# Rotary embedding, 16 x 512 x 1024: loading x ahead of the tables, and the last tile computed and stored in four pieces

## Chip, cores, metric

The kernel runs on one core of a Trainium2 chip. The metric is device time in microseconds (us); the other cores are idle. The profile's span (the length of the profiled execution) is some 2 us shorter than the time.

## The reference

```python
x = x.reshape(batch, seq, num_heads, head_dim)        # 16, 512, 16, 64, float32
x1, x2 = x[..., :half_dim], x[..., half_dim:]         # half_dim = 32
cos = cos[None, :, None, :]; sin = sin[None, :, None, :]   # 512 x 32 each
return np.concatenate([x1 * cos - x2 * sin, x1 * sin + x2 * cos], axis=-1)
```

It reads 33.6 MB of x, writes as much, and does little arithmetic on each element.

## The kernel before

Each of the 16 batches is one tile: 128 partitions x 4096 elements, four rows of x to a partition (J = 4). SyncE (SP) issues the loads, ScalarE (ACT) casts x to bf16 and issues the stores, VectorE (DVE) does two bf16 multiplies (by cos, by sin), a subtract and an add that write fp32.

```python
xpool: bufs=3   xbpool: bufs=2   mpool: bufs=2   opool: bufs=3      # abridged
nc.sync.dma_start(out=cos_f, in_=cos_v)
nc.scalar.dma_start(out=sin_f, in_=sin_v)
nc.vector.tensor_copy(out=cos_b, in_=cos_f)      # to bf16
nc.vector.tensor_copy(out=sin_b, in_=sin_f)
# ... cut: views ...
for b in range(batch):
    xt = xpool.tile([P, F], fp32, name="xt")
    nc.sync.dma_start(out=xt, in_=x_v[b])
    xb = xbpool.tile([P, F], bf16, name="xb")
    nc.scalar.copy(out=xb, in_=xt)
    # m1, m2 (bf16) and ot (fp32) are allocated
    nc.vector.tensor_tensor(out=full_view(m1), in0=full_view(xb), in1=bcast(cos_b), op=MULT)
    nc.vector.tensor_tensor(out=full_view(m2), in0=full_view(xb), in1=bcast(sin_b), op=MULT)
    nc.vector.tensor_tensor(out=half_view(ot, 0), in0=half_view(m1, 0), in1=half_view(m2, 1), op=SUB)
    nc.vector.tensor_tensor(out=half_view(ot, 1), in0=half_view(m1, 1), in1=half_view(m2, 0), op=ADD)
    nc.scalar.dma_start(out=out_v[b], in_=ot)
```

The program text does not fix the order in which ACT gets its casts and stores. The framework that builds the program arranges them (called the built order below).

## Time and profile before

| | before |
|---|---|
| time, median of 5 runs | 168.29 us (168.24 to 168.73) |
| span of the profiled run | 166.5 us |
| DVE / ACT busy | 142.4 / 58.9 us |
| moved by DMA | 67.25 MB, 404 GB/s over the span |

DVE is busy for 86% of the span, and the DMA engines are full from about 2 to 148 us, at 429 GB/s from 4 us on. The lines are in the prediction.

### The profile page before, as it was taken

The page shows a single profiled execution, that of the slowest core. Times are in us where ns is not written, and L with a number is a line of the kernel's source. Part 1 is how long each engine was busy: PE and PEld are TensorE (multiplying, and loading weights), DVE is VectorE, ACT ScalarE, POOL GpSimd, SP SyncE. Part 2 cuts the span into 40 slices and gives each one's busy share as a digit, 9 for nine tenths or more (in the row PEclk, how much of TensorE's full clock was granted, in tenths as well). Part 3 has the DMA queues.
Part 4 walks back from the last instruction along what each step waited for, and adds up shares of the span by engine and source line. Part 5 has one row for each costly group of instructions (what it writes and reads, how often), then busy time and mean ns, then how long its engine had stood idle before and what let it go on. Part 6 is the DMA issues. An engine that isn't in the chain of part 4 may idle for free.

```text
span 166.5 us, 216 instructions
## 1 busy us (share of the span) xinstructions
DVE 142.4 (86%) x66; ACT 58.9 (35%) x17; POOL 0.2 (0%) x4
## 2 busy tenths in 40 slices
DVE  0009999999999998199999999999999999999920
ACT  3076646153440000978080700533526080800000
POOL 0000000000000000000000000000000000000000
DMA  5999999999999999999999999999999999997455
GB/s 157 429 433 429 429 425 370 433 441 429 421 417 441 441 433 441 429 409 429 441 441 433 429 441 401 437 439 433 437 429 417 425 441 441 433 386 323 189 252 252
DMA packets 4897, 67.25 MB, mean 404 GB/s; under 512 B 544, under 2 KB 800, under 8 KB 800
## 3 DMA queue, kind: packets, MB, share of 16 engines
q1 hardware_dynamic: 2448, 33.62, 48.0%
q10 hardware_dynamic: 2448, 33.62, 47.3%
q14 instruction: 1, 0.01, 0.0%
HBM read 33.69 MB, written 33.55 MB: 404 GB/s over the span
## 4 chain that ended last, share of the span: by engine, by line
DVE 71%; issue 13%; DMA 5%; ACT 4%; DVEq 1%; SPq 0%; ACTq 0%
DVE ot L92 19%; DVE ot L86 19%; DVE m L80 17%; DVE m L83 16%; DMA xt<-in_x_dram 5%; ACT xb L74 4%; DVEq L129 1%; SPq L49 0%; ACTq L98 0%; DVEq L86 0%; ACTq L74 0%
## 5 line engine op out<-in xcount | busy, mean ns | idle before, releaser
L74 ACT CAST xb<-xt 128x4096 bf16<-128x4096 f32 x16 | 57.6, 3605 | 85.5 <-DVE ot L92 50.5
L80 DVE TENSOR_TENSOR m<-xb,cos_b 128x4096 bf16<-128x4096 bf16 x16 | 36.6, 2285 | 13.6 <-ACT xb L74 13.6
L86 DVE TENSOR_TENSOR ot<-m,m 128x2048 f32<-128x2048 bf16 x16 | 36.6, 2289 | 0.3
L92 DVE TENSOR_TENSOR ot<-m,m 128x2048 f32<-128x2048 bf16 x16 | 36.6, 2285 | 0.0
L83 DVE TENSOR_TENSOR m<-xb,sin_b 128x4096 bf16<-128x4096 bf16 x16 | 36.6, 2284 | 0.0
L53 DVE CAST cos_b<-cos_f 128x128 bf16<-128x128 f32 x1 | 0.2, 227 | 2.9 <-DMA cos_f<-in_cos_dram 2.9
L74 ACT ACT_TABLE_LOAD x1 | 1.3, 1283 | 1.1 <-PEq L115 1.1
L54 DVE CAST sin_b<-sin_f 128x128 bf16<-128x128 f32 x1 | 0.2, 228 | 0.0
L115 POOL MEMSET const-bfloat16-1.0<- 128x1 bf16 x1 | 0.1, 101 | 0.0
L115 POOL MEMSET const-uint8-127<- 128x1 uint8 x1 | 0.1, 101 | 0.0
L115 POOL MEMSET const-float32-0.0<- 128x1 f32 x1 | 0.1, 98 | 0.2 <-issue 0.2
L115 POOL MEMSET const-float32-1.0<- 128x1 f32 x1 | 0.1, 98 | 0.0
## 6 DMA issues: line engine op xcount, KB each, us to landing
xt<-in_x_dram SPq DMA_DIRECT2D x16, 2048.0 KB, 18.9
out_dram<-ot ACTq DMA_DIRECT2D x16, 2048.0 KB, 14.8
sin_f<-in_sin_dram ACTq DMA_DIRECT2D x1, 64.0 KB, 2.3
cos_f<-in_cos_dram SPq DMA_DIRECT2D x1, 64.0 KB, 2.1
```

The source lines that it names most:

```text
L53: nc.vector.tensor_copy(out=cos_b, in_=cos_f)
L54: nc.vector.tensor_copy(out=sin_b, in_=sin_f)
L74: nc.scalar.copy(out=xb, in_=xt)
L80: nc.vector.tensor_tensor(out=full_view(m1), in0=full_view(xb), in1=bcast(cos_b), op=MULT)
L83: nc.vector.tensor_tensor(out=full_view(m2), in0=full_view(xb), in1=bcast(sin_b), op=MULT)
L86: nc.vector.tensor_tensor(out=half_view(ot, 0), in0=half_view(m1, 0), in1=half_view(m2, 1), op=SUB,)
L92: nc.vector.tensor_tensor(out=half_view(ot, 1), in0=half_view(m1, 1), in1=half_view(m2, 0), op=ADD,)
L115: nc = _bacc.Bacc("TRN2", target_bir_lowering=False, num_devices=1)
L129: with _tile.TileContext(nc) as tc:
```

## The change

It parametrizes the kernel (J and the buffer counts are unchanged: 4; 3, 2, 2, 3) and is meant to have two effects: the first x load is issued ahead of the cos load, so that the first cast may start sooner, and the last tile is computed and stored in four pieces, so that most of its store lies beside its arithmetic. The diff, cut to these (the comments are added here):

```diff
-    nc.sync.dma_start(out=cos_f, in_=cos_v)
-    nc.scalar.dma_start(out=sin_f, in_=sin_v)
+    pending = load_x(*plan[0])          # the first x load
+    build_tables(Jt_first)              # cos on SP, sin on ACT, and their casts
+    build_tables(J)                     # J = Jt_first = 4: returns at once
...
+        if i == len(plan) - 1:
+            for j in range(J):
+                def piece(v, j=j):
+                    return v[:, j:j + 1]
+                TT = nc.vector.tensor_tensor
+                TT(out=piece(full_view(m1, Jt)), in0=piece(full_view(xb, Jt)), in1=bcast(cb[Jt][t][:, j * half:(j + 1) * half], 1), op=MULT)
+                TT(out=piece(full_view(m2, Jt)), in0=piece(full_view(xb, Jt)), in1=bcast(sb[Jt][t][:, j * half:(j + 1) * half], 1), op=MULT)
+                TT(out=piece(half_view(ot, 0, Jt)), in0=piece(half_view(m1, 0, Jt)), in1=piece(half_view(m2, 1, Jt)), op=SUB)
+                TT(out=piece(half_view(ot, 1, Jt)), in0=piece(half_view(m1, 1, Jt)), in1=piece(half_view(m2, 0, Jt)), op=ADD)
+                nc.scalar.dma_start(out=out_v[b, t][:, j * dim:(j + 1) * dim], in_=ot[:, j * dim:(j + 1) * dim])
+            continue
```

More of the change, by code (lines that the diff above doesn't have):

```diff
@@ L7 @@
 from concourse._compat import with_exitstack
+J = 4
+X_BUFS = 3
+XB_BUFS = 2
+M_BUFS = 2
+O_BUFS = 3
 @with_exitstack
@@ L31 @@
     P = nc.NUM_PARTITIONS
-    assert seq % P == 0
-    J = seq // P
-    F = J * dim
-    x_v = x.rearrange("b (p j) k -> b p (j k)", j=J)
-    out_v = out.rearrange("b (p j) h d -> b p (j h d)", j=J)
-    cos_v = cos.rearrange("(p j) d -> p (j d)", j=J)
-    sin_v = sin.rearrange("(p j) d -> p (j d)", j=J)
-    consts = ctx.enter_context(tc.tile_pool(name="consts", bufs=1))
-    xpool = ctx.enter_context(tc.tile_pool(name="xpool", bufs=3))
-    xbpool = ctx.enter_context(tc.tile_pool(name="xbpool", bufs=2))
@@ L44 @@
-    mpool = ctx.enter_context(tc.tile_pool(name="mpool", bufs=2))
-    opool = ctx.enter_context(tc.tile_pool(name="opool", bufs=3))
-    cos_f = consts.tile([P, J * half], fp32, name="cos_f")
-    sin_f = consts.tile([P, J * half], fp32, name="sin_f")
-    nc.sync.dma_start(out=cos_f, in_=cos_v)
-    nc.scalar.dma_start(out=sin_f, in_=sin_v)
-    cos_b = consts.tile([P, J * half], bf16, name="cos_b")
-    sin_b = consts.tile([P, J * half], bf16, name="sin_b")
-    nc.vector.tensor_copy(out=cos_b, in_=cos_f)
@@ L54, with make_views @@
-    nc.vector.tensor_copy(out=sin_b, in_=sin_f)
-    def bcast(t):
+    assert seq % (P * J) == 0
+    nst = seq // (P * J)
+    def make_views(Jt):
+        x_v = x.rearrange("b (t p j) k -> b t p (j k)", p=P, j=Jt)
+        out_v = out.rearrange("b (t p j) h d -> b t p (j h d)", p=P, j=Jt)
+        cos_v = cos.rearrange("(t p j) d -> t p (j d)", p=P, j=Jt)
+        sin_v = sin.rearrange("(t p j) d -> t p (j d)", p=P, j=Jt)
+        return x_v, out_v, cos_v, sin_v
+    consts = ctx.enter_context(tc.tile_pool(name="consts", bufs=1))
@@ new lines, with build_tables @@
+    xpool = ctx.enter_context(tc.tile_pool(name="xpool", bufs=X_BUFS))
+    xbpool = ctx.enter_context(tc.tile_pool(name="xbpool", bufs=XB_BUFS))
+    mpool = ctx.enter_context(tc.tile_pool(name="mpool", bufs=M_BUFS))
+    opool = ctx.enter_context(tc.tile_pool(name="opool", bufs=O_BUFS))
+    xv = {}
+    cb = {}
+    sb = {}
+    def build_tables(Jt):
+        if Jt in cb:
+            return
+        x_v, out_v, cos_v, sin_v = make_views(Jt)
+        xv[Jt] = (x_v, out_v)
+        n_t = seq // (P * Jt)
+        cb[Jt] = []
+        sb[Jt] = []
+        for t in range(n_t):
+            cf = consts.tile([P, Jt * half], fp32, name=f"cos_f{Jt}_{t}")
+            sf = consts.tile([P, Jt * half], fp32, name=f"sin_f{Jt}_{t}")
+            nc.sync.dma_start(out=cf, in_=cos_v[t])
+            nc.scalar.dma_start(out=sf, in_=sin_v[t])
+            cbt = consts.tile([P, Jt * half], bf16, name=f"cos_b{Jt}_{t}")
+            sbt = consts.tile([P, Jt * half], bf16, name=f"sin_b{Jt}_{t}")
+            nc.vector.tensor_copy(out=cbt, in_=cf)
+            nc.vector.tensor_copy(out=sbt, in_=sf)
+            cb[Jt].append(cbt)
+            sb[Jt].append(sbt)
@@ L57, in bcast @@
+    def bcast(t, Jt):
         return bass.AP(
@@ L59, in bcast, with full_view, half_view @@
             offset=t.offset,
-            ap=[list(t.ap[0]), [half, J], [0, nh * 2], [1, half]],
+            ap=[list(t.ap[0]), [half, Jt], [0, nh * 2], [1, half]],
         )
-    def full_view(t):
-        return t.rearrange("p (j e d) -> p j e d", j=J, e=2 * nh, d=half)
-    def half_view(t, which):
-        v = t.rearrange("p (j h two d) -> p j h two d", j=J, h=nh, two=2)
+    def full_view(t, Jt):
+        return t.rearrange("p (j e d) -> p j e d", j=Jt, e=2 * nh, d=half)
+    def half_view(t, which, Jt):
+        v = t.rearrange("p (j h two d) -> p j h two d", j=Jt, h=nh, two=2)
@@ L68, in half_view, with schedule @@
         return v[:, :, :, which, :]
-    for b in range(batch):
-        xt = xpool.tile([P, F], fp32, name="xt")
-        nc.sync.dma_start(out=xt, in_=x_v[b])
-        xb = xbpool.tile([P, F], bf16, name="xb")
-        nc.scalar.copy(out=xb, in_=xt)
-        m1 = mpool.tile([P, F], bf16, name="m1")
-        m2 = mpool.tile([P, F], bf16, name="m2")
-        ot = opool.tile([P, F], fp32, name="ot")
+    def schedule(Jt_first):
+        seq_tiles = []
+        for b in range(batch):
+            Jt = Jt_first if b == 0 else J
+            n_t = seq // (P * Jt)
+            for t in range(n_t):
+                seq_tiles.append((b, Jt, t))
+        return seq_tiles
@@ new lines, with load_x @@
+    Jt_first = 4
+    plan = schedule(Jt_first)
+    def load_x(b, Jt, t):
+        x_v = make_views(Jt)[0]
+        xt = xpool.tile([P, Jt * dim], fp32, name="xt")
+        nc.sync.dma_start(out=xt, in_=x_v[b, t])
+        return xt
+    pending = load_x(*plan[0])
+    build_tables(Jt_first)
+    build_tables(J)
+    for i, (b, Jt, t) in enumerate(plan):
+        Ft = Jt * dim
+        out_v = xv[Jt][1]
+        xt = pending if i == 0 else load_x(b, Jt, t)
+        xb = xbpool.tile([P, Ft], bf16, name="xb")
+        nc.scalar.copy(out=xb, in_=xt)
+        m1 = mpool.tile([P, Ft], bf16, name="m1")
+        m2 = mpool.tile([P, Ft], bf16, name="m2")
+        ot = opool.tile([P, Ft], fp32, name="ot")
+        if i == len(plan) - 1:
[9 more added lines that the diff above has]
+            continue
@@ L80 @@
         nc.vector.tensor_tensor(
-            out=full_view(m1), in0=full_view(xb), in1=bcast(cos_b), op=MULT
+            out=full_view(m1, Jt), in0=full_view(xb, Jt), in1=bcast(cb[Jt][t], Jt), op=MULT
         )
         nc.vector.tensor_tensor(
-            out=full_view(m2), in0=full_view(xb), in1=bcast(sin_b), op=MULT
+            out=full_view(m2, Jt), in0=full_view(xb, Jt), in1=bcast(sb[Jt][t], Jt), op=MULT
         )
         nc.vector.tensor_tensor(
-            out=half_view(ot, 0),
-            in0=half_view(m1, 0),
@@ L89 @@
-            in1=half_view(m2, 1),
+            out=half_view(ot, 0, Jt),
+            in0=half_view(m1, 0, Jt),
+            in1=half_view(m2, 1, Jt),
             op=SUB,
@@ L92 @@
         nc.vector.tensor_tensor(
-            out=half_view(ot, 1),
-            in0=half_view(m1, 1),
-            in1=half_view(m2, 0),
+            out=half_view(ot, 1, Jt),
+            in0=half_view(m1, 1, Jt),
+            in1=half_view(m2, 0, Jt),
             op=ADD,
         )
-        nc.scalar.dma_start(out=out_v[b], in_=ot)
+        nc.scalar.dma_start(out=out_v[b, t], in_=ot)
 _INS = ['x', 'cos', 'sin', 'num_heads']
```

## The prediction

> **What bounds the kernel now.** I read the page first, for shares of the span, then the chain of waits and the instruction timeline, because shares of a whole run hide stages. The diff keeps the tile (J is 4 before and after, so each of the 16 batches is still one 128x4096 tile) and all buffer counts. So only three places can change: the start, the order in which the engines get their instructions, and the last tile.
>
> ```profile
> DVE 142.4 (86%) x66; ACT 58.9 (35%) x17; POOL 0.2 (0%) x4
> DVE  0009999999999998199999999999999999999920
> DMA  5999999999999999999999999999999999997455
> ```
> These are lines of the page. VectorE (DVE) has work from slice 3 (12.8 us) on with one hole at slice 16, and the DMA engines are full from the second slice to about 150 us. Both are near their limit. The last slices differ: DVE has stopped and DMA is at about half. That is one transfer with nothing beside it.
>
> ```profile
> L74 ACT CAST xb<-xt 128x4096 bf16<-128x4096 f32 x16 | 57.6, 3605 | 85.5 <-DVE ot L92 50.5
> L80 DVE TENSOR_TENSOR m<-xb,cos_b 128x4096 bf16<-128x4096 bf16 x16 | 36.6, 2285 | 13.6 <-ACT xb L74 13.6
> L86 DVE TENSOR_TENSOR ot<-m,m 128x2048 f32<-128x2048 bf16 x16 | 36.6, 2289 | 0.3
> ```
> These groups give a tile's cost: four DVE operations of about 2.29 us each. DVE idles 13.6 us before L80: 9.5 at the start (the first cast) and 4.1 in the middle.
>
> ```profile
> 1.15 8.01 DMA xt<-in_x_dram
> 9.18 3.61 ACT xb L74
> 12.82 2.29 DVE m L80
> ```
> These, from the chain that ended last, are the start: the first x load, the first cast, the first multiply. The load is issued at 1.15, after the cos load's issue (0.73 to 1.10 on the same queue), and lands 8.0 us later. Cos and sin landed by 3.05 us and were not waited for by the multiply.
>
> ```profile
> 63.85 2.28 DVE L92 TENSOR_TENSOR ot<-m,m 128x2048 f32<-128x2048 bf16 x1
> 66.60 7.11 ACT L74 CAST xb<-xt 128x4096 bf16<-128x4096 f32 x2 [19.06 <-DVE ot L92]
> 70.24 2.29 DVE L80 TENSOR_TENSOR m<-xb,cos_b 128x4096 bf16<-128x4096 bf16 x1 [4.11 <-ACT xb L74]
> ```
> This is the hole, from the timeline. The x load of that tile was issued at 29.95 us, and no load took over 23.2 us, so its data had long landed; its buffer was free at about 52.7. The cast stands behind two stores in ACT's queue, and the second waits for the last DVE operation of the tile before. So it is the order of ACT's instructions, fixed when the kernel is built, that costs 4.1 us. From 70.24 on DVE never waits again.
>
> ```profile
> 148.06 2.29 DVE L92 TENSOR_TENSOR ot<-m,m 128x2048 f32<-128x2048 bf16 x1
> 150.27 2.28 DVE L80 TENSOR_TENSOR m<-xb,cos_b 128x4096 bf16<-128x4096 bf16 x1
> 150.38 9.27 ACTq L98 DMA_DIRECT2D out_dram<-ot  x2
> 152.47 2.28 DVE L83 TENSOR_TENSOR m<-xb,sin_b 128x4096 bf16<-128x4096 bf16 x1
> 154.79 2.29 DVE L86 TENSOR_TENSOR ot<-m,m 128x2048 f32<-128x2048 bf16 x1
> 157.00 2.29 DVE L92 TENSOR_TENSOR ot<-m,m 128x2048 f32<-128x2048 bf16 x1
> ```
> This is the end: the last tile's four operations run to 159.28 and only then is its whole 2 MB store issued. Its landing time is the shortest of all stores, 6.3 us, so it lands at 165.6, and the span ends 0.9 us later. Windows of the trace say that DMA moved nothing from 156 to 160 us and then 2.1 MB. So the end is bound by DVE and then by an exposed store.
>
> **What the Trainium skill says.** First, VectorE: DVE Perf Modes, section "The TRN2 errata", says that an operation on SBUF data pays a fixed cost per instruction, and gives (N+151)/0.96 ns for an fp32 tensor_tensor. For N = 2048 that is 2291 ns; the page here has 2289, so it agrees. The timeline adds that an independent next operation starts about 0.08 us before the end of the one ahead (148.06 + 2.29 = 150.35 against 150.27), and one that needs the result just made starts about 0.03 us after (152.47 + 2.28 = 154.75 against 154.79). Second, DMA: Bandwidth & Descriptors, section "Anatomy of one DMA", fits about 2.0 us plus bytes at 436 GB/s, for the GpSimd path. For 2.1 MB that is 6.8 us; the lone last store took 6.3, so the fixed part here looks nearer 1.4. Third, the same page, "Queues, rings and completion order": each engine takes a queue's descriptors in ring order. So a cos load issued behind x would arrive at about the time of x; the trace of before has it the other way round and cannot show this. Fourth, Perfetto Trace Analysis, "DMA Optimizations": splitting a DMA may let some of it start sooner if the DMA engines are idle. They are, from 156 to 160 us.
>
> **The change part by part.** (a) The start: x is issued first and cos behind it. The x load moves from 1.15 to 0.73 us, 0.42 earlier. The cos load should land about when x does, near 9 us, and its two casts of 0.23 us each then lie beside ACT's 3.6 us cast of x, so nothing new is waited for. The whole DVE chain follows by 0.42, since later loads have slack: only the first three casts ever waited for a load. Worth -0.4.
>
> (b) The middle: the same instructions, shapes and buffers. Worth 0 if ACT's order stays.
>
> (c) The last tile on DVE: 16 operations of a quarter size instead of 4. By the skill's formula with N = 512 (bf16 multiplies count two per cycle: 1024/2 = 512) each lasts (512+151)/0.96 = 691 ns, and the next starts after 0.61 if independent and after 0.72 if it needs the one just before. Tile 15 starts at 150.27 - 0.42 = 149.85. If another piece's multiply is put between the sin multiply and the subtract (the order before does this between tiles, at 23.96 to 28.36 us), only the last subtract waits: 14 x 0.61 + 0.72 + 0.69 = 9.95 us. If not, 11 x 0.61 + 4 x 0.72 + 0.69 = 10.28 us. DVE ends at 159.8 to 160.1, say 159.95: 0.7 us later than before, in spite of the earlier start.
>
> (d) The last store: four of 0.52 MB. The store of tile 14 is issued at about 150 and empties by about 156. Pieces 0 to 2 come ready about every 2.5 us (153, 155, 158) and need some 1.2 us each at 430 GB/s, so they are out before piece 3. Piece 3 is alone. Its landing, an estimate: 6.3 us less 1.57 MB at 430 GB/s (3.66) = 2.64; with the skill's fixed part of 2.0 it is 3.2. I take 2.75, as the 64 KB cos load took 2.1 and so the fixed part is no larger than that. End: 159.95 + 0.03 + 2.75 + 0.9 = 163.6, against 166.5: -2.9. In time: 168.29 - 2.9 = 165.4 us, which is 1.7% faster.
>
> **The rivals.** First, the built order changes. Moving the cos load and adding 12 operations may lead the scheduler to another order of casts and stores on ACT. The profile can't say which. If the 4.1 us hole disappears, DVE ends that much earlier; the DMA engines have then to move 67.25 MB at some 430 GB/s, 156 us from 2 us on, so a little of it is lost to DMA: 161 to 162 us. If a second such hole opens, 169. For a steady order speaks that tiles 1 to 14 are written as before; against it, that a hole like this one depends on which of two instructions was ready first in the plan. I give 15% to a better and 7% to a worse order.
>
> Second, the split stores may be held up: if the store of a piece were taken to read the whole output tile, the next piece's subtract would wait for it, and compute and transfer would run in turn, 4 x (2.5 + 2.7) = 21 us after 149.85: 172 us in the trace and 173.5 in time. Against it: L86 and L92 write interleaved halves of one tile, and L92 starts 0.08 us before L86 ends, so disjoint parts are not held apart. 3%.
>
> Third, the quarter-size operations may cost more than thought, or 4 KB rows of a store move more slowly than the 16 KB rows of before. Each 0.1 us per operation is 1.6 us. That would leave 166 to 167 us.
>
> Fourth, the cos load may land after the first cast ends (12.4 us). It would have to take over 11 us for its 64 KB; x's 2 MB take 8. Unlikely, and worth at most 1 us.
>
> **Range and chances.** With the order unchanged (78%) I expect 164.8 to 166.2, centre 165.4; the 2% line is at 164.9, so some 15% of that case is beyond it. Adding nearly all of the better order's 15% gives 0.27 for faster by over 2%, 0.05 for slower and 0.68 between. The 80% range, stretched to the fast side for the first rival, is 162.8 to 166.7.
>
> **What would show it right or wrong.** Right: the first x load issued near 0.73 and the first multiply at about 12.4; the hole of some 4 us before a cast still there at about 66 us; 16 operations of about 690 ns at the end and DVE finishing near 160; four stores of 512 KB with the last landing in 2.6 to 3.2 us. Wrong: a missing or second hole (first rival), subtracts that wait for DMA in the last tile (second), pieces well over 0.7 us (third), or a wait for cos before the first multiply (fourth).

## The result, and the profile after

The changed kernel takes 163.25 us (median of 8 runs, 163.16 to 163.31) against 168.73 (15 runs, 168.24 to 169.37; the five of the table above are among them). The ratio is 0.9678, 95% interval 0.9662 to 0.9694: faster by 3.2%. Ratios in this document are the mean time of one kernel's fast runs over that of the other's in the same rounds, so they are not quite the ratio of the medians quoted.

First the page of the changed kernel: the same three rows as shown of before.

```profile
DVE 143.5 (89%) x78; ACT 59.0 (37%) x17; POOL 0.2 (0%) x4
DVE  0019999999999999999999999999998997999990
DMA  5999999999999999999999999999999999999994
```

The hole of DVE at slice 16 is gone, and the DMA row is full to its last slice but one. There are new small dips of DVE late, at slices 30 and 33 (counted from 0). The view of waits names them (who waited for whom: us in total, times, longest):

```profile
DVE m L137 <- ACT xb L119: 3.0, 1, 3.0
DVE ot L143 <- DMA out_dram<-ot: 1.6, 2, 0.8
```

DVE's only wait for a cast is now the first; in its place come two waits for a store to free an output buffer. Before had no such wait.

The start, from the chain that ended last (start, us, what):

```profile
0.73 8.02 DMA xt<-in_x_dram
8.75 0.02 issue
8.78 3.61 ACT xb L119
12.39 0.02 issue
12.41 2.29 DVE m L137
```

The load takes 8.02 us, as before, from an issue 0.42 us earlier, and the first multiply moves from 12.82 to 12.41.

Where the hole was, from the timeline (start, us, engine, line, operation):

```profile
57.38 3.61 ACT L119 CAST xb<-xt 128x4096 bf16<-128x4096 f32 x1 [5.33 <-DVE ot L149]
...
63.56 2.29 DVE L149 TENSOR_TENSOR ot<-m,m 128x2048 f32<-128x2048 bf16 x1
65.77 2.28 DVE L137 TENSOR_TENSOR m<-xb,cos_b 128x4096 bf16<-128x4096 bf16 x1
```

The cast that this multiply needs was done at 61.0, long before the tile ahead of it was finished. In the built program ACT's queue has another order (c5 is the cast of tile 5, s5 its store; tiles are numbered from 0):

```
before:  c0 c1 c2 s0 c3 s1 c4 s2 c5 s3 s4 s5 c6 c7 c8 s6 c9 s7 c10 s8 s9 c11 s10 c12 ...
after:   c0 c1 c2 s0 c3 s1 c4 s2 s3 c5 s4 c6 s5 c7 s6 c8 s7 c9 s8 c10 s9 c11 s10 c12 ...
```

Before, c6 stood behind s5, which waits for all of tile 5 on DVE; so DVE had nothing of tile 6 when it finished tile 5. After, c6 stands behind s4. The starts of casts and stores in ACT's timelines of both traces follow these two orders.

The end, from the timeline:

```profile
147.71 0.68 DVE L130 TENSOR_TENSOR m<-xb,cos_b 128x1024 bf16<-128x1024 bf16 x1
147.82 0.34 ACTq L155 DMA_DIRECT2D out_dram<-ot  x1
...
150.83 7.09 ACTq L134 DMA_DIRECT2D out_dram<-ot  x4
...
155.53 0.69 DVE L131 TENSOR_TENSOR m<-xb,sin_b 128x1024 bf16<-128x1024 bf16 x1
156.25 0.69 DVE L132 TENSOR_TENSOR ot<-m,m 128x512 f32<-128x512 bf16 x1
156.86 0.68 DVE L133 TENSOR_TENSOR ot<-m,m 128x512 f32<-128x512 bf16 x1
```

The last tile takes 147.71 to 157.54, 9.83 us. Independent operations start 0.60 us apart (147.71 to 148.31); only the last subtract, which nothing could be put in front of, starts 0.72 after the one ahead. The four issues stretch from 150.83 to 157.92. Two windows of the changed trace (the columns are window, its length, busy us and instructions of DVE, ACT and POOL, clock, DMA share, GB/s):

```profile
148.00:156.00 8.00, 8.00 (x14) 0.00 (x0) 0.00 (x0) 1.00 0.99 419
156.00:158.00 2.00, 1.51 (x3) 0.00 (x0) 0.00 (x0) 1.00 1.00 408
```

The 4 us without a transfer, 156 to 160 us in the trace of before, are filled.

So three things moved together: the start, the order on ACT, and the last tile.

### The profile page after: what moved, and what is told of

Read it like the earlier page. It is cut to its first block, busy times and chain, and to the rows that moved or that the text cites. A ratio compares the mean times of both kernels' runs of the same rounds, so it can differ in the third digit from the quotient of the medians.

```text
span 161.5 us, 230 instructions
## 1 busy us (share of the span) xinstructions
DVE 143.5 (89%) x78; ACT 59.0 (37%) x17; POOL 0.2 (0%) x4
## 3 DMA queue, kind: packets, MB, share of 16 engines
q1 hardware_dynamic: 2448, 33.62, 49.4%
## 4 chain that ended last, share of the span: by engine, by line
DVE 67%; DMA 20%; issue 8%; ACT 2%; DVEq 0%
DVE ot L143 18%; DVE m L140 15%; DVE ot L149 15%; DMA out_dram<-ot 15%; DVE m L137 12%; DMA xt<-in_x_dram 5%; ACT xb L119 2%; DVE ot L132 2%; DVE m L130 2%; DVE m L131 2%; DVE ot L133 1%; DVEq L186 0%; DVEq L143 0%
## 5 line engine op out<-in xcount | busy, mean ns | idle before, releaser
L137 DVE TENSOR_TENSOR m<-xb,cos_b 128x4096 bf16<-128x4096 bf16 x15 | 34.3, 2285 | 3.0 <-ACT xb L119 3.0
L143 DVE TENSOR_TENSOR ot<-m,m 128x2048 f32<-128x2048 bf16 x15 | 34.4, 2291 | 2.0 <-DMA out_dram<-ot 1.6
L149 DVE TENSOR_TENSOR ot<-m,m 128x2048 f32<-128x2048 bf16 x15 | 34.3, 2285 | 0.0
L140 DVE TENSOR_TENSOR m<-xb,sin_b 128x4096 bf16<-128x4096 bf16 x15 | 34.3, 2285 | 0.0
L132 DVE TENSOR_TENSOR ot<-m,m 128x512 f32<-128x512 bf16 x4 | 2.7, 686 | 0.0
L131 DVE TENSOR_TENSOR m<-xb,sin_b 128x1024 bf16<-128x1024 bf16 x4 | 2.7, 685 | 0.0
L133 DVE TENSOR_TENSOR ot<-m,m 128x512 f32<-128x512 bf16 x4 | 2.7, 684 | 0.0
L130 DVE TENSOR_TENSOR m<-xb,cos_b 128x1024 bf16<-128x1024 bf16 x4 | 2.7, 684 | 0.0
```

The source lines that it names most:

```text
L130: TT(out=piece(full_view(m1, Jt)), in0=piece(full_view(xb, Jt)), in1=bcast(cb[Jt][t][:, j * half:(j + 1) * half], 1), op=MULT)
L131: TT(out=piece(full_view(m2, Jt)), in0=piece(full_view(xb, Jt)), in1=bcast(sb[Jt][t][:, j * half:(j + 1) * half], 1), op=MULT)
L132: TT(out=piece(half_view(ot, 0, Jt)), in0=piece(half_view(m1, 0, Jt)), in1=piece(half_view(m2, 1, Jt)), op=SUB)
L133: TT(out=piece(half_view(ot, 1, Jt)), in0=piece(half_view(m1, 1, Jt)), in1=piece(half_view(m2, 0, Jt)), op=ADD)
L137: nc.vector.tensor_tensor(out=full_view(m1, Jt), in0=full_view(xb, Jt), in1=bcast(cb[Jt][t], Jt), op=MULT)
L140: nc.vector.tensor_tensor(out=full_view(m2, Jt), in0=full_view(xb, Jt), in1=bcast(sb[Jt][t], Jt), op=MULT)
```

## The experiments

**Theory.** The gain is the sum of an earlier start (0.4 us), another order on ACT that closes the hole (and is a side effect of moving the load), and a last store that is hidden. The closed hole, 4.1 us of DVE, is not worth 4.1 us, because DVE then meets the limit of the DMA engines. **Rivals.** The split changed the order; or the earlier load itself closes the hole; or DVE still bounds the changed kernel. The first four runs were taken together, against 168.27 us of before (11 runs).

### Split alone

The kernel of before with the last tile in pieces (the diff's loop), cos still first. In the built program ACT's order up to the pieces is that of before.

> Only the last tile is split; cos is still loaded first, and the built order of casts and stores on ACT is that of before. Theory (the gain is a sum of two parts: the exposed last store, and the hole that the moved load closes): the hole of about 4.1 us near 66 us stays; the last tile starts at 150.3, takes 9.8 us as in the changed kernel, its last store lands in about 2.7 us, span 163.7, 2.8 us less than before (ratio about 0.983). Rival (the order of ACT was changed by the split): the hole is gone and most of the 5 us gain is here (ratio about 0.968).

165.72 us, ratio 0.9851 (0.9829 to 0.9873); span 163.7. From its timeline and from the view of its output's stores:

```profile
66.29 7.11 ACT L82 CAST xb<-xt 128x4096 bf16<-128x4096 f32 x2 [19.05 <-DVE ot L112]
69.92 2.29 DVE L100 TENSOR_TENSOR m<-xb,cos_b 128x4096 bf16<-128x4096 bf16 x1 [4.11 <-ACT xb L82]
```
```profile
DMA to landing us min/median/max: 2.6/14.7/19.5
```

The hole of 4.11 us is there and the last piece lands in 2.6 us. The split is worth 1.5% by itself and did not change the order.

### x first alone

```diff
+    xt0 = xpool.tile([P, F], fp32, name="xt")
+    nc.sync.dma_start(out=xt0, in_=x_v[0])
     nc.sync.dma_start(out=cos_f, in_=cos_v)
...
+        if b == 0:
+            xt = xt0
+        else:
```

> Only x is loaded ahead of cos; the last tile is whole. In the built program ACT's casts and stores stand in the order of the changed kernel. Theory: no hole at 66 us; DVE ends near 156.6 with some 1.6 us of waits for output buffers, the last 2 MB store is exposed for 6.3 us, span about 163.8, 2.7 us less than before (ratio about 0.984). Rival (moving the load is worth only its 0.4 us of issue): ratio 0.997.

165.76 us, ratio 0.9836 (0.9812 to 0.9860); span 164.0. No hole; DVE's waits for an output buffer are 1.7 us, and the whole last store is exposed again (6.3 us to landing). A move of one issue by 0.4 us gives 1.6%.

### The new order alone

The kernel of before, cos first and the last tile whole, with edges between instructions (order only, no wait) that hold ACT's queue in the order of the changed kernel.

```diff
+    order = "c0 c1 c2 s0 c3 s1 c4 s2 s3 c5 s4 c6 s5 c7 ...".split()
+    for one, two in zip(order, order[1:]):
+        one, two = act[one[0], int(one[1:])], act[two[0], int(two[1:])]
+        tc.add_manual_dep(two.ins, one.ins.name, mybir.DependencyInfo(
+            mybir.DependencyClass.NoSync, mybir.DependencyReason.DATA), reason="act order")
```

> The kernel of before with cos first and the last tile whole, but ACT's casts and stores forced into the order of the changed kernel. Theory (the order is what closes the hole, not the earlier issue): nearly all of the gain of the run with x first, about 0.4 us less of it: span about 164.2, ratio about 0.986. Rival (the earlier start shifts the loads so that the hole closes by itself): ratio 1.00.

166.16 us, ratio 0.9872 (0.9850 to 0.9894). Its profiled execution has a span of 164.8, of which some 0.7 us is a first x load that landed later than in the profile of before (first cast at 9.90 against 9.18). No hole; two waits for output buffers, 1.5 us. The order by itself, with no load moved, is worth 1.3%.

### x first with the old order

The kernel with x first alone, with ACT's queue held in the order of before.

> x is loaded ahead of cos, the last tile is whole, and ACT's casts and stores are forced into the order of before. Theory: the hole of 4.1 us stays, everything starts 0.4 us earlier: 0.4 us less than before, ratio 0.9975. Rival (the earlier load is what counts): ratio about 0.984, as with x first alone.

168.03 us, ratio 0.9980 (0.9963 to 0.9996). The hole is back:

```profile
69.83 2.29 DVE L86 TENSOR_TENSOR m<-xb,cos_b 128x4096 bf16<-128x4096 bf16 x1 [4.10 <-ACT xb L80]
```

So the earlier issue is worth about 0.2 to 0.4 us, and the rest of what x first brought is the order. By the ratios: 1.5% (split) + 1.3% (order) + 0.2% (earlier issue) = 3.0%, against the measured 3.2%; each of the three has an uncertainty of about 0.2%.

### Less DVE work in the changed kernel

The next three runs shared the runs of before (168.38 us). Here ACT's order is held, and in tiles 4 to 11 a copy stands in place of the sin multiply; the result is wrong.

```diff
-        nc.vector.tensor_tensor(out=full_view(m2, Jt), in0=full_view(xb, Jt), in1=bcast(sb[Jt][t], Jt), op=MULT)
+        if 4 <= i < 12:
+            nc.vector.tensor_copy(out=m2, in_=xb)
+        else:
+            ...  # as before
```

> The changed kernel with its ACT order held, and in tiles 4 to 11 a plain bf16 copy in place of the sin multiply (wrong result on purpose), which should take about 1.2 us in place of 2.3 and so about 9 us of DVE work away. Theory (the changed kernel is at the limit of the DMA engines, 67.26 MB at about 430 GB/s from 2 us on, which is 156 us): DVE waits for buffers or data instead, and the span falls by at most 1.5 us. Rival (DVE is still the bound): the span falls by about 8 us, to 153 to 154.

163.33 us, against 163.25 of the changed kernel (of other rounds; the ratios to before are 0.9703 here and 0.9678 there, whose intervals overlap; the next run, of the same rounds as this one and with all of its DVE work, took 163.31). The copy took 1.22 us, so 8.5 us of DVE work are gone (135.0 busy in place of 143.5), and the time did not move. Its waits:

```profile
DVE ot L148 <- DMA out_dram<-ot: 10.3, 7, 1.9
```

1.6 us of waiting for output buffers have become 10.3: 8.7 us more, all that was saved. DVE does not bound the changed kernel.

### Four output buffers

`O_BUFS = 4` in the changed kernel; nothing else.

> The changed kernel with four output buffers in place of three. Theory (DMA is the limit): DVE's two waits for an output buffer (1.6 us) go and DVE ends near 156, but the stores left over queue and the end moves by 0.5 us or less. Rival (DVE and its waits set the end): 1.6 us less, span 159.9.

163.31 us, ratio 0.9706 (0.9691 to 0.9720). The two waits are gone and DVE finishes at about 156, but the pieces of the last store now take 5.8 us to land (median) where they took 4.1. What waits is only moved from DVE to the queue of stores.

### First tile in pieces

A try for a faster version: cos and sin first again, the first tile loaded, cast and computed in four pieces, four output buffers, and a regular order on ACT (c0 c1 s0 c2 s1 c3 s2 ...).

```diff
+        if b == 0:
+            for j in range(J):
+                jj = slice(j * dim, (j + 1) * dim)
+                nc.sync.dma_start(out=xt[:, jj], in_=x_v[b, t][:, jj])
...
+                if i == 0:
+                    nc.scalar.copy(out=xb[:, jj], in_=xt[:, jj])
```

> The changed kernel with cos and sin ahead again, the first tile loaded, cast and computed in four pieces, four output buffers and a regular order on ACT; a try for a faster version. DVE can start near 5 us in place of 12.4. Theory (DMA is the limit): the 7 us are lost to waits for loads and buffers, and the span falls by 0.5 to 1.5 us to about 160 to 161. Rival (DVE is the limit): the span falls by over 5 us.

164.27 us, ratio 0.9766 (0.9744 to 0.9788): 1.0 us slower than the changed kernel, where the theory expected a small gain. DVE starts at 7.2 (not near 5, as expected) and ends at 155.1 us, earlier than in any other kernel with the right result, and it doesn't help, which speaks for the DMA limit. The direction of the small difference was a miss. Two windows of its trace:

```profile
2.00:4.00 2.00, 0.41 (x2) 0.45 (x1) 0.00 (x0) 1.00 0.95 199
4.00:6.00 2.00, 0.00 (x0) 0.00 (x0) 0.00 (x0) 1.00 0.93 338
```

From 2 to 6 us the DMA engines are marked as busy but move 199 and 338 GB/s, against 281 and 442 in the same windows of before (0.37 MB less); these are the tables and the first 512 KB pieces. The kernel to compare with is the changed one: its windows from 0 to 6 us add up to 1.48 MB and those of this run to 1.11, again 0.37 MB less. At 430 GB/s that is an estimated 0.9 us of a DMA-bound kernel, about what was lost. Whether the small rows or the order of the loads is to blame was not taken apart.

### Fewer bytes, then both cuts

The last two runs shared runs of before at 168.32 us. Both hold ACT's order and store only half of each of tiles 4 to 11, so 8.4 MB less; the second also has the copy in place of the sin multiply. Their outputs are wrong, which doesn't matter for the times.

```diff
-        nc.scalar.dma_start(out=out_v[b, t], in_=ot)
+        kk = slice(0, (Ft // 2 if 4 <= i < 12 else Ft))
+        nc.scalar.dma_start(out=out_v[b, t][:, kk], in_=ot[:, kk])
```

> The changed kernel with its ACT order held, and only half of each of tiles 4 to 11 stored (wrong result on purpose): 8.4 MB less, which is 19.5 us of DMA at 430 GB/s. Theory (DMA and DVE are within about 2 us of each other in the changed kernel): DVE's two waits for output buffers (1.6 us) go, DVE ends near 155.9 and bounds at once, the last store lands 2.6 us after: span about 159.5, 2 us less. Rival (DMA alone bounds, DVE has much room): far more than 2 us less.

161.71 us, ratio 0.9604 (0.9587 to 0.9621), span 159.8. 19.5 us of transfers (8.4 MB at 430 GB/s) are taken away and the time falls by 1.5 (against 163.25 of other rounds): DVE never waits for an output buffer any more, and bounds at once. Its row on the page:

```profile
DVE  0019999999999999999999999999999999999990
```

> Both cuts at once: the copy in place of the sin multiply in tiles 4 to 11 (8.5 us of DVE work) and half of the stores of these tiles. Theory: now the DVE cut counts in full, DVE ends near 147.4, span about 151, 10.5 us less than the changed kernel. Rival (something else, as the casts or the order on ACT, holds the kernel near 161 us): the span stays above 158.

153.40 us, ratio 0.9105 (0.9092 to 0.9119), span 151.6: 9.9 us less than the changed kernel. The same DVE cut that was worth nothing alone is now worth 161.71 - 153.40 = 8.3 us of its 8.5. Page rows of this run:

```profile
DVE 135.0 (89%) x78; ACT 59.0 (39%) x17; POOL 0.2 (0%) x4
DVE  0016999999999999999999999999999999999990
```

So in the changed kernel DMA bounds, and DVE is only 1.5 us behind. With both cuts the casts and their order do not hold the kernel up: after the start DVE never waits for one. No version tried beats the changed kernel with the right result.

## Why the prediction was right or wrong

The time lay in the range (162.8 to 166.7), but the case that the prediction held most likely, an unchanged order with 164.8 to 166.2 us, is not what happened: the time lies in the range because the range was stretched for the first rival. By its steps:

- **(a) The start, -0.4 us: right.** The multiply started at 12.41, as worked out; the cos load landed at 9.1 us, behind x, and nothing waited for it. The run with x first and the old order measured it alone: ratio 0.9980.
- **(b) The middle, "Worth 0 if ACT's order stays": the step that failed.** It was given 78%, and the order did not stay. Moving the load, which (a) valued at 0.4 us, also changed where the builder put the casts, and that was worth 1.3%. The first rival named this and its sign, with 15%. Its working was right that the hole is one of order: the order alone closes it. Its figure, "161 to 162 us", was too low by 1.3 to 2.3 us.
- **The mis-sized term of that rival** is "a little of it is lost to DMA". The last tile without the hole would have started at 149.85 - 4.11 = 145.74 and did at 147.71: half of the 4.1 us was lost, 1.6 of it, by the view of waits, to the two waits for output buffers. The run with four output buffers, which has no such waits, starts the last tile at 146.18; what is left, about 0.4 us, is of the size of what the new DVE order costs: four fewer subtracts (two in place of six) have a multiply of the next tile put ahead of them, at about 0.12 us each. But that run is no faster, so these waits do not set the end; the transfers do. The rival took 156 us of transfers "from 2 us on", which ends at 158. In the trace of the changed kernel the last bytes move shortly before 160 and the last store lands at 160.5. By its windows, DMA moved 0.58 MB in the first 4 us, where 430 GB/s from 2 us on would be 0.86, and 417 GB/s from 148 to 158 us; from 158.0 to 158.5, just after the last piece was issued, it moved 123 GB/s. No run takes these apart.
- **(c) The last tile, 9.95 us if interleaved: right**, 9.83 measured, operations of 684 to 686 ns against 691.
- **(d) The last store: right in size.** "6.3 us less 1.57 MB at 430 GB/s" gave 2.64, and the run with the split alone shows 2.6 (the prediction's "nearer 1.4" for the fixed part of the lone 2 MB store was a slip: 6.3 us less the 4.8 that 2.1 MB take at the 436 GB/s used there is 1.5); in the changed kernel, where the engines are still full until 158 us, it is 2.9. The split was worth 1.5% where (c) and (d) with no earlier start would give about 2.5 us, 1.5%.
- **The other rivals** did not occur: no subtract of the last tile waited for a store, no operation was slow, and the cos load came in time.

Had the rival's chance been higher, the forecast would have been better. The profile did show the risk: a hole that depends on an instruction order which the text does not fix. What would have settled it is not in a profile but in the built program.

## What to carry to other kernels

When a framework orders an engine's queue, even a small edit can reorder it far away from the edit: compare the built queues of both versions before giving a gain to the line that was changed, and hold the order with explicit edges to measure it. On an engine that issues stores, which wait for the last operation of a tile, the next tile's cast belongs ahead of that store, not behind it. And where two units are both near their limit, cut the work of each and of both in turn: here 8.5 us of DVE work was worth 0, 19.5 us of transfers 1.5, and both together 9.9.

## What the Trainium skill lacked or had wrong

- DMA: Bandwidth & Descriptors, "Queues, rings and completion order": it says that an engine takes turns between queues, packet by packet. The 64 KB sin load, alone on ACT's queue and issued at 0.73 us, the same time as x on SP's, took 8.2 us to land here; with x issued 0.4 us later, as before, it took 2.3. In every run here with x issued first it took 8.1 us or more. The page says that an engine drains a whole packet of one queue, some 9 to 17 descriptors as a rule, before it turns to the next, but not how much of a load issued from SP or ACT is one packet. The profile counts 144 packets to a transfer here (2448 for the 17 on SP's queue), 9 for each of the 16 engines. If these are the page's descriptors, all of an x load may be one packet to an engine, and the sin load would stand behind it; no run tested this.
- The same page, "Anatomy of one DMA" (fitted for the GpSimd path): 2.0 us plus bytes at 436 GB/s gives an estimated 3.2 us for a 0.52 MB store and 6.8 for 2.1 MB. Stores with nothing beside them, issued from ACT, landed in 2.6 and 6.3 us, so the fixed part was 1.4 to 1.5. The page has no such fit for loads and stores issued from SP or ACT.
- The same page, "Bandwidth": its table of measured rates is for loads only, issued from GpSimd, with 425 GB/s for 16 MB on a core whose neighbour is idle. With loads and stores mixed, issued from SP and ACT, and one core running, 429 GB/s (before) and 430 (changed) were held from 4 to 148 us.
- VectorE: DVE Perf Modes, "The TRN2 errata": (N+151)/0.96 is right for a duration to 1% (691 ns against 684 to 686 at N = 512). What adds up on a busy engine is the distance of starts: 0.60 us at N = 512 and 2.20 at N = 2048 when independent, 0.72 and 2.32 when an operation needs the one ahead. The section's 58 + N cycles, an estimated 0.594 and 2.194 us, which it sets aside as too low for a duration, fits these independent starts well; the section doesn't say so.
- No page says what the order that the builder gives an engine's queue can cost: it was worth 1.3% here, and one moved load changed it.
